# First values accumulated in the projection's banks, and the second head begun beside the first

## The chip, the cores and the metric

The kernel runs on one core of one Trainium2 chip. TensorE (PE in the profile) multiplies into PSUM; VectorE (DVE), ScalarE (ACT) and GpSimd (POOL) read PSUM or SBUF and do everything else; SyncE (SP) issues the transfers. Each engine takes its instructions strictly in the order of its own queue, and semaphores tie the queues together. The metric is the time of one execution in device microseconds; less is better. The kernel before takes 2423.03 us (median of three runs, 2422.2 to 2424.73).

## What is computed

Two layers of a transformer trunk over 512 latent tokens and 256 context tokens, 1024 features wide. Only the start of the first layer matters here:

```python
mx = (silu_c @ w_ada[i] + b_ada[i])             # modulation: shift, scale, gate (latent)
mc = silu_cc @ w_ada[i] + b_ada[i]              # the same for the context
hc = modulate(rmsnorm(h_ctx, norm1_g[i]), sc1, ac1)
hx = modulate(rmsnorm(x, norm1_g[i]), sx1, ax1)
px = hx @ w_in[i]                               # columns: conv | q | k | v | gates
q_x = apply_rope(rmsnorm(q_x, q_norm_g[i]), cos, sin)     # per head, two maps of 64
k_x = apply_rope(rmsnorm(k_x, k_norm_g[i]), cos, sin)
# attention: two softmax maps per head (8 heads), p1 - lam * p2, times the values
```

Context tokens get the norm but no rotation. After attention, a convolution branch, a merge, an output projection and an MLP follow, and then the second layer.

## The kernel before

Every matmul is made of three, so that float32 accuracy comes out of rounded operands: each operand is split into a rounded high part and a remainder (`split`, lines 75 to 77: ACT rounds, line 76; DVE or POOL subtracts, line 77), and `mm3` (lines 102 to 106) accumulates high*high, high*low and low*high. In the rows of the trace these are the lines L104, L105 and L106. Tokens lie in six tiles of 128: tiles 0 to 3 are latent, 4 and 5 context (`NTT` is 6). Features lie in eight tiles of 128 (`KT` is 8, index `k`).

**The prologue.** The input is normalized and transposed (L324, L329, L331), and the modulation weights come in slabs of 1 MB (`ada_slab`, L209 on: products L216 into `adaps`, copy L222, turn L225, reductions L228, bias L231; `ada_gain` is L240). The loop over `q` takes two slabs at a time, 4+q and q, which give shift and scale of the feature tiles 2q and 2q+1. For these two the modulated input is formed (L368 into `XN`) and split into `h1h` and `h1l`. `qk_part(k)` then accumulates the first head's queries and keys for feature tile `k` over all six token tiles. Each token tile has a PSUM bank of 512 float32 columns, `ps_qk[t]`, of which queries and keys use the left 256. Behind the loop the first value slab is loaded (`v_slab`, pair 0: heads 0 and 1), with its remainder subtracted on POOL, and the residual stream `X` is copied out to `xs_d` (3 MB) behind that load.

**The heads.** `qk_head(h)` is a generator. For each token tile, `project(t)` makes the matmuls (none for head 0, which takes `ps_qk`) and then copies the raw result out of its bank (L488, `rw`), squares it (L491, `sq`), reduces (DVE L493), adds epsilon and takes the power -1/2 on POOL (L494, L495), scales the keys (L496: DVE for latent tiles, POOL for context), and rotates: on POOL L505 (`ra`) and L509 (`rb`, two), added on DVE at L513 into `dup`; for context tiles POOL writes `dup` at L518. `turn(t)` transposes `dup` on PE (L529, `qkT`), copies it (ACT L533) and subtracts remainders (DVE L534, L536). `v_pair(pr)` makes the values of two heads, token tile by token tile, each with 24 matmuls into a bank of its own, and splits the result into `vh` and `vl`. `attend(h)` makes scores (L658, L660: `S`), their maxima (DVE L662), exponentials (ACT L667) and so on.

The order of the first layer's head phase is written by hand: two steps of head 0, two of the values, then four rounds of head 0, values, head 0. Then, for each head, `merge` interleaves `attend(h)` with fill work in a given ratio: the next head's `qk_head` and part of the next pair of values. For h = 0, four steps of head 1 are drawn ahead of it. On top of this program order a scheduler arranges instructions on each engine; the order quoted below is the one after that.

## Time and profile before

| what | value |
|---|---|
| median of three runs | 2423.03 us |
| the profiled execution | 2429.01 us |
| its span, first to last instruction | 2427.0 us |
| mean granted TensorE clock | 0.985 |
| PE, DVE, ACT, POOL busy | 96%, 56%, 39%, 29% |
| first value matmul begins; second score tile of head 1 begins | 60.92 us; 144.35 us |

The span's 2427.0 us and 2.0 us around it make the 2429.01 us of the profiled execution. All times inside the trace are counted from the start of the span. A row of a timeline gives start, duration, engine, line and operation, and in brackets the idle time of that engine just before, with what ended it. Instructions of a kind that follow each other closely stand in one row with their count.

### The profile page before, as it was taken

The numbers are of one execution on the slowest core, as the hardware profiler recorded it, in microseconds if no ns is written. First come the engines' busy times: TensorE is split into PE (matmuls) and PEld (weight loads), VectorE is DVE, ScalarE is ACT, GpSimd is POOL, SyncE is SP. The second block draws the span as 40 slices with busy tenths as digits, with TensorE's granted clock in tenths as the row PEclk, the third lists the DMA queues.
The fourth block names the chain that finished last, engine by engine and source line by source line (L and its number), as shares of the span: only waits on it lengthen the run. The fifth ranks groups of instructions, "written<-read, shape, count | busy, mean of one in ns | idle before, by whom it ended". The sixth has DMA issues, their size and how long they took to land.

```text
span 2427.0 us, 36997 instructions
## 1 busy us (share of the span) xinstructions
PE 2329.8 (96%) x15034; PEld 2065.2 (85%) x15034; DVE 1347.6 (56%) x2311; ACT 948.0 (39%) x1839; POOL 693.7 (29%) x1034
## 2 busy tenths in 40 slices
PE   7999998999999999999999998999999989999999
PEld 6889998878878988888888997999977769888887
DVE  6666776499657452222222356676759966433332
ACT  5455665522323242221312245555552323422331
POOL 2856765120000131120211256675630000200100
PEclk9999999999999999999999998999998999999999
DMA  8201101144445133333333221111114323232322
GB/s 291 68 27 44 45 27 60 42 134 128 155 135 172 53 105 112 114 122 116 110 122 101 69 75 53 42 42 43 43 59 137 126 70 122 87 103 89 104 87 70
DMA packets 222186, 224.79 MB, mean 93 GB/s; under 512 B 5872, under 2 KB 212160, under 8 KB 221888
## 3 DMA queue, kind: packets, MB, share of 16 engines
q1 hardware_dynamic: 222016, 222.43, 28.6%
q8 instruction: 118, 1.93, 0.3%
q14 instruction: 52, 0.43, 0.1%
HBM read 208.73 MB, written 13.67 MB: 92 GB/s over the span
## 4 chain that ended last, share of the span: by engine, by line
PE 79%; POOL 8%; DVE 7%; ACT 3%; issue 1%; DMA 1%; SPq 0%; POOLq 0%; ACTq 0%; DVEq 0%
PE r L104 6%; PE r L106 6%; PE f L104 6%; PE r L105 6%; PE f L105 6%; PE f L106 6%; PE gt L104 3%; PE gt L106 3%; PE gt L105 3%; PE adaps L216 2%; PE qk L104 2%; PE qk L105 2%; PE yc L113 2%; PE qk L106 2%; PE o L104 2%; PE o L106 2%
## 5 line engine op out<-in xcount | busy, mean ns | idle before, releaser
L104 PE MATMUL r<-fh,h_w 128*128 128x512 f32 (+1 forms) x832 | 285.5, 344 | 0.5 <-DVE X L1082 0.5
L104 PE MATMUL f<-h2h,h_w 128*128 128x512 f32 (+1 forms) x832 | 284.3, 345 | 1.3 <-ACT h2h L76 1.0
L105 PE MATMUL f<-h2l,h_w 128*128 128x512 f32 (+1 forms) x832 | 284.1, 343 | 1.1 <-POOL h2l L77 1.0
L105 PE MATMUL r<-fl,h_w 128*128 128x512 f32 (+1 forms) x832 | 283.2, 341 | 0.0
L106 PE MATMUL r<-fh,l_w 128*128 128x512 f32 (+1 forms) x832 | 283.2, 341 | 0.0
L106 PE MATMUL f<-h2h,l_w 128*128 128x512 f32 (+1 forms) x832 | 282.3, 341 | 0.0
L76 ACT ACTIVATE h_w<-r_w 128x1024 fp32r<-128x1024 f32 x128 | 128.8, 1053 | 312.4 <-PE r L105 131.0
L1151 POOL TENSOR_TENSOR fr<-fr 128x512 f32<-128x512 f32 (+1 forms) x104 | 93.3, 899 | 508.2 <-ACT fh L1150 508.2
L897 DVE SCALAR_TENSOR_TENSOR cacc<-z,cols,cacc 128x783 f32<-128x783 f32 (+1 forms) x240 | 203.7, 902 | 0.4
L104 PE MATMUL qk<-h_wqk,h1h 128*128 128x256 f32 x640 | 184.7, 291 | 7.8 <-ACT h1h L76 3.6
L105 PE MATMUL qk<-l_wqk,h1h 128*128 128x256 f32 x640 | 182.1, 286 | 0.0
L1082 DVE SCALAR_TENSOR_TENSOR X<-r,ad,X 128x512 f32<-128x512 f32 (+1 forms) x104 | 64.9, 627 | 210.3 <-PE r L106 210.2
L106 PE MATMUL qk<-h_wqk,h1l 128*128 128x256 f32 x640 | 178.7, 287 | 0.0
L104 PEld LDWEIGHTS f<-h2h,h_w 128*128 128x128 f32 x832 | 157.4, 190 | 25.0 <-ACT fh L1150 2.5
L104 PEld LDWEIGHTS r<-fh,h_w 128*128 128x128 f32 x832 | 157.6, 190 | 23.7 <-issue 3.7
L105 PEld LDWEIGHTS f<-h2l,h_w 128*128 128x128 f32 x832 | 158.3, 190 | 20.6 <-POOL h2l L77 2.5
L667 ACT ACTIVATE e<-S,st,rqk 128x768 f32<-128x768 f32 (+1 forms) x160 | 145.0, 909 | 75.5 <-POOL st L664 72.6
L106 PEld LDWEIGHTS f<-h2h,l_w 128*128 128x128 f32 x832 | 158.1, 190 | 17.6
L106 PEld LDWEIGHTS r<-fh,l_w 128*128 128x128 f32 x832 | 157.7, 190 | 17.8
L105 PEld LDWEIGHTS r<-fl,h_w 128*128 128x128 f32 x832 | 157.8, 190 | 17.0
L77 DVE TENSOR_TENSOR l_w<-r_w,h_w 128x1024 fp32r<-128x1024 f32 x106 | 126.2, 1223 | 79.5 <-ACT h_w L76 77.8
L1152 DVE TENSOR_TENSOR fl<-fr,fh 128x512 fp32r<-128x512 f32 (+1 forms) x104 | 62.5, 604 | 189.3 <-POOL fr L1151 189.2
(248 smaller groups left out, 6280.7 us busy)
## 6 DMA issues: line engine op xcount, KB each, us to landing
r_w<-in_w_mlp_dram SPq DMA_DIRECT2D x64, 1024.0 KB, 5.3
ada<-in_w_ada_dram SPq DMA_DIRECT2D x48, 1024.0 KB, 5.3
r_wqk<-in_w_in_dram SPq DMA_DIRECT2D x32, 512.0 KB, 5.2
r_wg<-in_w_in_dram SPq DMA_DIRECT2D x16, 1024.0 KB, 5.3
r_wv<-in_w_in_dram SPq DMA_DIRECT2D x8, 1024.0 KB, 5.4
r_wao<-in_w_attn_out_dram SPq DMA_DIRECT2D x8, 1024.0 KB, 5.2
r_wo<-in_w_out_dram SPq DMA_DIRECT2D x8, 1024.0 KB, 8.3
at_d<-uo SPq DMA_DIRECT2D x40, 128.0 KB, 1.7
```

The costliest lines, as they stand in the source:

```text
L76: nc.scalar.activation(out=hi, in_=src, func=AF.Copy)
L77: (lo_eng or nc.vector).tensor_tensor(out=lo, in0=src, in1=f32(hi), op=ALU.subtract)
L104: nc.tensor.matmul(ps, sh, mh, start=first, stop=False)
L105: nc.tensor.matmul(ps, sh, ml, start=False, stop=False)
L106: nc.tensor.matmul(ps, sl, mh, start=False, stop=last)
L113: nc.tensor.matmul(ps, w[j][:, k, m0 : m0 + P], a(k)[0][:, toks], start=k + j == 0, stop=False)
L216: nc.tensor.matmul(ps[32 * j : 32 * j + 32, :256], cvec[:, k, :], r[:, k, :], start=k < 4, stop=k >= 4, tile_position=(0, 32 * j))
L667: nc.scalar.activation(out=e[:, :nkey], in_=S[:, :nkey], func=AF.Exp, scale=R[:, t, m : m + 1], bias=st[:, m : m + 1], accum_out=st[:, 2 + ...
L897: nc.vector.scalar_tensor_tensor(out=ca[cc][:, :CV], in0=zt[cc][:, t : t + CV], scalar=wcol, in1=ca[cc][:, :CV], op0=ALU.mult, op1=ALU.add)
L1082: nc.vector.scalar_tensor_tensor(out=X[:, mb, g], in0=ps[:, :W], scalar=gate[:, s, mb : mb + 1], in1=X[:, mb, g], op0=ALU.mult, op1=ALU.add)
L1151: nc.gpsimd.tensor_tensor(out=r[:, :W], in0=r[:, :W], in1=r[:, :W], op=ALU.mult)
L1152: nc.vector.tensor_tensor(out=fl[mb][:, g], in0=r[:, :W], in1=f32(fh[mb][:, g]), op=ALU.subtract)
```

## The change

There are two parts.

First, the values of pair 0 are no longer made tile by tile in banks of their own. Their slab is loaded inside the modulation loop at q = 2, ahead of that turn's two modulation slabs. A new function `v_part` accumulates them, feature tile by feature tile, in the right half of the six banks `ps_qk[t]`, whose left half holds head 0's queries and keys: feature tiles 0 and 1 behind projection parts 4 and 5, the other six behind parts 6 and 7. Since the projection's first matmul has opened the bank, these begin with `start=False`. `v_pair(0)` then only splits the right halves into `vh` and `vl`.

Second, head 1's generator is made ahead of the hand-written order and four of its steps (three projections and more) are drawn there, one in each round where a tile of values stood; the loop over heads takes this generator on.

```diff
+    def v_part(ks):
+        w = first["v"]
+        for k in ks:
+            for t in range(NTT):
+                for a, b, e in ((hh, 0, False), (hh, 1, False), (hl, 0, k == KT - 1)):
+                    nc.tensor.matmul(ps_qk[t][:, 256:], a[:, k, t * P : t * P + P], w[b][:, k, :],
+                                     start=False, stop=e, skip_group_check=True)
+
     for q in range(4):
+        if q == 2:
+            first["v"] = v_slab(0, 0, nc.gpsimd)
         ada_slab(0, L, 4 + q)
         ada_slab(0, L, q)
...
             qk_part(2 * q - 1)
+        if q == 3:
+            v_part(range(2))
     qk_part(KT - 2)
     qk_part(KT - 1)
+    v_part(range(2, KT))
     first["ps"], first["w"] = ps_qk, w_qk
-    first["v"] = v_slab(0, 0, nc.gpsimd)
...
         def v_pair(pr):
+            pre = ps_qk if i == 0 and pr == 0 else []
...
             for t in range(NTT):
+                if pre:
+                    split(vh[:, t], vl[:, t], pre[t][:, 256:])
+                    yield 0.0
+                    continue
                 ps = mm_tile(f"v{i}_{pr}_{t}")
...
-            drain(part(head0, 2))
-            drain(part(v0, 2))
+            head1 = qk_head(1)
+            for _ in range(2):
+                drain(part(head0, 1))
+                drain(part(v0, 1))
             for _ in range(NTT - 2):
                 drain(part(head0, 1))
                 drain(part(v0, 1))
+                drain(part(head1, 1))
                 drain(part(head0, 1))
...
-                qk = qk_head(h + 1)
+                qk = head1 if h == 0 and not last else qk_head(h + 1)
```

The lines behind the new function move by 12 to 19 in the changed kernel: L368 becomes L380, L488 to L536 become L502 to L550, L658 becomes L677, L660 becomes L679. The value matmuls of pair 0 are L369.

On SP, the queue of loads at the end of the modulation, before:

```order
L81 DMA ada_1_410<-in_w_ada_dram 128x8x256
L81 DMA ada_6_478<-in_w_ada_dram 128x8x256
L81 DMA ada_2_496<-in_w_ada_dram 128x8x256
L81 DMA ada_7_564<-in_w_ada_dram 128x8x256
L81 DMA ada_3_582<-in_w_ada_dram 128x8x256
L90 DMA r_wv_0_686<-in_w_in_dram 128x8x256
L379 DMA xs_d_79<-X_92 128x6144
L88 DMA r_wqk_1_991<-in_w_in_dram 128x8x128 x2
```

and now:

```order
L81 DMA ada_1_410<-in_w_ada_dram 128x8x256
L90 DMA r_wv_0_478<-in_w_in_dram 128x8x256
L81 DMA ada_6_486<-in_w_ada_dram 128x8x256
L81 DMA ada_2_504<-in_w_ada_dram 128x8x256
L393 DMA xs_d_79<-X_92 128x6144
L81 DMA ada_7_572<-in_w_ada_dram 128x8x256
L81 DMA ada_3_590<-in_w_ada_dram 128x8x256
L88 DMA r_wqk_1_903<-in_w_in_dram 128x8x128 x2
```

The value slab passes four modulation slabs, and the copy of the residual passes the last two.

On POOL, from the split of the value slab on, before (`rqk` is the norm of a head's tiles, `l_` a weight's remainder; the first number in a name is the head, the next the tile):

```order
L77 TENSOR_TENSOR l_wv_0_689<-r_wv_0_686,h_wv_0_688 128x1024 x2
L494 TENSOR_SCALAR rqk_0_705<-rqk_0_705 128x4
L495 TENSOR_TENSOR rqk_0_705<-rqk_0_705,mhalf 128x4
L505 TENSOR_TENSOR ra_0_0_715<-rw_0_0_706,tC_120 128x256
L509 TENSOR_TENSOR rb_0_0_716<-rw_0_0_706,tS_121 128x4x32 x2
```

and now:

```order
L77 TENSOR_TENSOR l_wv_0_481<-r_wv_0_478,h_wv_0_480 128x1024 x2
L77 TENSOR_TENSOR l_wqk_1_907<-r_wqk_1_903,h_wqk_1_906 128x1024
L508 TENSOR_SCALAR rqk_0_849<-rqk_0_849 128x4
L509 TENSOR_TENSOR rqk_0_849<-rqk_0_849,mhalf 128x4
L77 TENSOR_TENSOR l_wv_1_1385<-r_wv_1_1382,h_wv_1_1384 128x1024
L519 TENSOR_TENSOR ra_0_0_859<-rw_0_0_850,tC_120 128x256
L523 TENSOR_TENSOR rb_0_0_860<-rw_0_0_850,tS_121 128x4x32 x2
```

The halves of head 1's projection weights and of the second value slab, which stood behind head 0's tiles 0 and 5, now stand ahead of and inside tile 0.

On PE, around the first scores, before (`qkT` are turns, `S` scores; head, tile):

```order
L106 MATMUL qk_1_1_1050<-h_wqk_1_994,h1l_335 128x256
L658 MATMUL S_0_0_0_1104<-qk_0_704 128x512
L660 MATMUL S_0_0_0_1104<-qk_0_704 128x512
L658 MATMUL S_0_0_1_1113<-qk_0_704 128x512
L660 MATMUL S_0_0_1_1113<-qk_0_704 128x512
L529 MATMUL qkT_0_4_1042<-cst,dup_0_4_900 128x128 x2
L529 MATMUL qkT_0_5_1090<-cst,dup_0_5_946 128x128 x4
L104 MATMUL qk_1_2_1127<-h_wqk_1_994,h1h_334 128x256
```

and now:

```order
L106 MATMUL qk_1_3_1124<-h_wqk_1_906,h1l_335 128x256
L543 MATMUL qkT_0_2_1080<-cst,dup_0_2_894 128x128 x4
L543 MATMUL qkT_1_0_1101<-cst,dup_1_0_947 128x128 x4
L543 MATMUL qkT_0_3_1109<-cst,dup_0_3_970 128x128 x4
L677 MATMUL S_0_0_0_1194<-qk_0_848 128x512
L679 MATMUL S_0_0_0_1194<-qk_0_848 128x512
L677 MATMUL S_0_0_1_1203<-qk_0_848 128x512
L679 MATMUL S_0_0_1_1203<-qk_0_848 128x512
L543 MATMUL qkT_0_4_1164<-cst,dup_0_4_1035 128x128 x2
L543 MATMUL qkT_1_1_1172<-cst,dup_1_1_1012 128x128 x4
```

Four projections of head 1 (tiles 0 to 3) and a turn of head 1 now stand ahead of the first scores, where two projections stood; head 0's turns 0_0 to 0_2, which lay among the value matmuls, come behind them. The rest of the first scores (the last 256 keys) stands behind the fifth projection, where it stood behind the third.

## The prediction

> **What bounds the kernel now.** I read the page's busy table and chain of waits first, then the table by stretches, and last the rows of the stretches that the change touches.
>
> ```profile
> span 2427.0 us, 36997 instructions
> PE 2329.8 (96%) x15034; PEld 2065.2 (85%) x15034; DVE 1347.6 (56%) x2311; ACT 948.0 (39%) x1839; POOL 693.7 (29%) x1034
> PE 79%; POOL 8%; DVE 7%; ACT 3%; issue 1%; DMA 1%; SPq 0%; POOLq 0%; ACTq 0%; DVEq 0%
> ```
>
> PE works 96% of the span, and the change leaves its matmuls as they are (13429 rows in both orders). So the change can only move the time in which PE waits. POOL is busy 29% on average, but it holds 8% of the chain: somewhere it sets the pace. The stretches say where (columns: PE, PEld, DVE, ACT, POOL busy, granted clock, DMA share, GB/s):
>
> ```profile
> 50.00:55.00 5.00, 2.91 (x25) 2.71 (x23) 4.90 (x7) 0.90 (x1) 4.70 (x2) 1.00 0.25 103
> 55.00:60.00 5.00, 3.54 (x29) 3.54 (x30) 3.69 (x9) 1.76 (x4) 0.00 (x0) 1.00 0.02 6
> 60.00:70.00 10.00, 10.00 (x85) 9.92 (x83) 4.76 (x7) 5.33 (x13) 6.67 (x8) 1.00 0.38 102
> 70.00:81.00 11.00, 9.77 (x83) 9.53 (x82) 7.98 (x18) 4.06 (x10) 9.44 (x15) 1.00 0.30 97
> 81.00:90.00 9.00, 7.93 (x61) 7.17 (x61) 4.23 (x8) 3.99 (x8) 8.76 (x11) 1.00 0.01 3
> 90.00:97.00 7.00, 5.98 (x35) 5.53 (x36) 3.50 (x9) 1.78 (x4) 5.81 (x9) 0.76 0.56 149
> 97.00:121.00 24.00, 22.32 (x174) 21.08 (x173) 21.29 (x41) 15.04 (x31) 20.81 (x37) 1.00 0.16 43
> 121.00:145.00 24.00, 23.12 (x185) 22.09 (x184) 13.10 (x29) 12.95 (x34) 6.64 (x21) 1.00 0.05 14
> ```
>
> From 62 to 121 us POOL is busy nearly throughout (9.44 of 11, 8.76 of 9, 20.81 of 24), and PE still loses only about 5 us there. PE is kept going because it has the first values' matmuls to do from 60.92 on, while POOL already normalizes and rotates head 0's tiles. The one large PE wait is in 50 to 60, and its cause stands in these rows of POOL, DVE, ACT and PE:
>
> ```profile
> 50.03 4.70 POOL L77 TENSOR_TENSOR l_wv<-r_wv,h_wv 128x1024 fp32r<-128x1024 f32 x2 [16.79 <-ACT h_wv L76]
> 50.14 2.31 DVE L231 TENSOR_TENSOR ad<-ad,cols 128x4 f32<-128x4 f32 x1
> 52.49 2.33 DVE L240 SCALAR_TENSOR_TENSOR A<-ad,cols 128x2 f32<-128x2 f32 x2
> 55.01 0.16 DVE L231 TENSOR_TENSOR ad<-ad,cols 128x4 f32<-128x4 f32 x1
> 56.47 0.39 PE L104 MATMUL qk<-h_wqk,h1h 128*128 128x256 f32 x1 [3.55 <-ACT h1h L76]
> 35.23 0.60 ACT L329 ACTIVATE XN<-nT 128x512 f32<-128x512 f32 x1 [0.79 <-PE nT L324]
> 37.19 0.17 DVE L231 TENSOR_TENSOR ad<-ad,cols 128x4 f32<-128x4 f32 x1
> ```
>
> A 128x4 add that takes 0.16 us takes 2.31 while POOL splits the wv slab, and the next DVE step waits for POOL's second half. PE then stands 3.55 us. The Trainium skill, "SBUF — State Buffer", section "Who interferes with whom", calls the port pair that VectorE and GpSimd share an exclusive lock; the trace agrees (4.70 us of POOL against 2.31 + 2.33 of DVE), and by that rule too an earlier split moves the block rather than ending it.
>
> **The change, part by part.** First, the early wv slab. Its load now stands where ada_6 stood. ACT's two h_wv halves come right behind its L329 copy (35.23 + 0.60), so POOL's split starts at about 37 and lasts to 41.7. DVE has just come to the L231 of the second modulation group (37.19). It is held to about 41.5, some 4.2 us late. PE has the ada_6 products ahead of what waits for this, so I take a PE wait of 3.9 us; bounds 0 and 4.7.
>
> The third group's wait was covered by the products of ada_7 and ada_3; these now come behind the value matmuls. The chain is in these rows:
>
> ```profile
> 45.16 0.38 PE L225 MATMUL adaps<-cst,adasb 128*128 128x128 f32 x2
> 45.92 0.16 DVE L231 TENSOR_TENSOR ad<-ad,cols 128x4 f32<-128x4 f32 x1
> 46.70 0.94 ACT L76 ACTIVATE h1h<-XN 128x512 fp32r<-128x512 f32 x2 [3.88 <-DVE XN L368]
> ```
>
> From the end of the turn (45.5) to the first half of h1h (about 47.3) it is 1.8 us, uncovered now. In the fourth group two turns stand side by side in front of the last projection parts, so the same chain with a second gain is some 2.4 us. I take 1.85 + 2.4; bounds 0 each and 4.4 together, or 9.1 with the first. The load of the residual copy also moves ahead of ada_7 and ada_3, but all of these bytes had landed soon after 50 us (the 50 to 55 row moves only 103 GB/s), and PE comes to those products at about 60: nothing.
>
> When do the values end? Rows of PE:
>
> ```profile
> 60.92 0.39 PE L104 MATMUL v<-h_wv,h1h 128*128 128x256 f32 x1
> 71.48 0.39 PE L104 MATMUL v<-h_wv,h1h 128*128 128x256 f32 x1 [1.23 <-DVE vl L77]
> 79.80 0.60 PE L529 MATMUL qkT<-cst,dup 128*128 128x128 f32 x4
> 80.95 0.28 PE L106 MATMUL v<-h_wv,h1l 128*128 128x256 f32 x1
> 88.14 0.40 PE L658 MATMUL S<-qk 128*128 128x512 f32 x1
> 96.46 0.28 PE L658 MATMUL S<-qk 128*128 128x256 f32 x1
> 144.35 0.50 PE L658 MATMUL S<-qk 128*128 128x512 f32 x1
> ```
>
> Before, the last value matmul gives way at 81.07. Three turns of head 0 lie among them (0.36 from one start to the next matmul, 1.1 in all), and the waits of 3.55 and 1.23. Without these it would be 75.2. With the new waits of 8.15 it is **83.3**. The prologue alone is thus no gain: 4.8 us of waiting goes, 8.15 comes.
>
> Second, and this carries the forecast: head 0's POOL work loses its cover. The copy of each tile out of its bank (raw q and k) now waits for the last matmul into that bank, and that is a value matmul. All six banks end within 1.8 us at 83.3, because the values run by feature tile. So POOL, which began head 0 at 62.62, begins at about 84. Its price per tile:
>
> ```profile
> 62.62 0.24 POOL L494 TENSOR_SCALAR rqk<-rqk 128x4 f32<-128x4 f32 x1 [7.88 <-DVE rqk L493]
> 62.94 1.03 POOL L495 TENSOR_TENSOR rqk<-rqk,mhalf 128x4 f32<-128x4 f32 x1
> 64.43 0.74 POOL L505 TENSOR_TENSOR ra<-rw,tC 128x256 f32<-128x256 f32 x1 [0.46 <-DVE rw L496]
> 65.14 0.88 POOL L509 TENSOR_TENSOR rb<-rw,tS 128x128 f32<-128x128 f32 x2
> 66.09 1.08 POOL L494 TENSOR_SCALAR rqk<-rqk 128x4 f32<-128x4 f32 x1
> 76.53 0.73 POOL L494 TENSOR_SCALAR rqk<-rqk 128x4 f32<-128x4 f32 x1
> 80.56 1.03 POOL L494 TENSOR_SCALAR rqk<-rqk 128x4 f32<-128x4 f32 x2
> 86.42 2.40 POOL L77 TENSOR_TENSOR l_wv<-r_wv,h_wv 128x1024 fp32r<-128x1024 f32 x1
> 89.14 0.72 POOL L518 TENSOR_TENSOR dup<-rw,gr 128x256 f32<-128x256 f32 x1
> 88.78 0.39 POOL L496 TENSOR_TENSOR rw<-rw,rqk 128x128 f32<-128x128 f32 x1
> ```
>
> A latent tile takes 3.47 (62.62 to 66.09) to 4.03 us (76.53 to 80.56); I take 3.7. POOL's new order is: norm of head 0's tile 0 (84.0 to 85.3); half of the second wv slab, for which ACT first rounds 2 us (86.5 to 88.9); the rest of tile 0 (to 90.6); then tiles 0_1, 0_2, 1_0, 0_3, 1_1, five at 3.7, to 109.1. Then context tile 0_4 mixed with 1_2: two L494 0.5, two L518 1.44, two L495 2.4, L496 0.4, L505 0.74, L509 0.88, in all 6.4; and 0_5 mixed with 1_3 up to its last dup, without the L509 pair, 5.5: **121.0**. Head 0's last turn, its copy and two differences take 0.3 + 0.6 + 0.85 by these rows:
>
> ```profile
> 84.23 0.60 ACT L533 ACTIVATE qk<-qkT 128x512 fp32r<-128x512 f32 x1 [0.67 <-PE qkT L529]
> 84.86 0.42 DVE L534 TENSOR_TENSOR qk<-qkT,qk 128x256 fp32r<-128x256 f32 x1 [0.65 <-ACT qk L533]
> ```
>
> So the last part of the first scores, at 96.46 before, comes at **122.8**, 26.3 later. PE has done more by then: the projections of head 1's tiles 3 and 4 (48 matmuls, 0.12 apart, 5.8) and three turns (1.1), 6.9 us that the later stretch no longer holds. Net 19.4. That PE has projections in this stretch does not help enough: from 83.3 it has four of them (11.5 us), the fourth behind a copy that stands on ACT behind head 0's first turn; the fifth stands behind the turns, and PE is in order. Of 39 us it works about 19.
>
> Third, what comes back: from 97 to 145 PE waits 2.6 us (24 - 22.32 and 24 - 23.12), partly for POOL, which has less left to do there. I take 2.4 back. From the second head's second score tile (144.35) on, the order is nearly the same, so what is late there stays late. **Sum: +19.4 - 2.4 = +17.** The profiled execution took 2429.0 (span 2427.0), 6 us above the median of the runs, so 2446 profiled and **2440** as a median.
>
> Least: the prologue's waits all hidden (-8.15) and tiles at 3.47 (-1.2), so +8. Most: waits of 9.1, tiles at 4.03 (+1.7), nothing regained, +24.
>
> **The rivals.** (1) Faster: head 1's projections cover head 0's chain, and the 36 value matmuls fill the wait of 3.55. Then PE loses neither 3.55 nor 1.23 nor the 2.1 it waits from 81 to 97: -6.9, 2416. It needs head 0's six tiles through POOL in the 11.5 us of four projections, under 2 us each, where no row shows less than 3.47. 8%.
>
> (2) The copies wait only for their own half of the bank. Then POOL starts when the last projection part ends, 60.92 - 3.55 + 8.15 + 4.3 (36 values) = 69.8, so at about 71.5 rather than 84, and the first scores come 12 us sooner: +5 to +7, 2429. For it: the two halves are different addresses. Against: copy and values use one bank tile, and the copy's wait in the order is on PE behind the values. 8%.
>
> (3) No change: POOL's idle time after 121 (6.64 busy of 24) takes up the delay. That holds for POOL, not for PE, whose score matmuls stand in order behind the turns. It needs PE waits of under 5 us in the head stretch. 8%.
>
> (4) The waiting slows the clock. In 90 to 97 the granted clock is 0.76, behind waits of a few tenths, yet 1.00 behind the wait of 3.55. If it fell in the starved stretch, the fifth projection and the turns ahead of the first scores (4 us of matmuls) would take up to twice as long: +4, 2444. [...] 13%.
>
> **How the numbers follow.** Forecast 63%: 2440, its own range 2430 to 2448. With the cases the range is 2428 to 2449: it leaves out rival 1, rival 3, and parts of the tails. A measurement of this kernel can tell about 0.2% (4.8 us) from no change. Faster 8%; same 10% (rival 3, and a piece of rival 2); slower 82%.
>
> **What would show it.** Right: POOL's first norm of head 0 at about 84 instead of 62.6; PE busy for only half of 84 to 122, its waits ended by DVE and POOL (dup, rw, qk); the last part of the first scores at 119 to 126; the score at 144.35 near 161; POOL's wv split near 37 with long DVE rows beside it, and PE's wait of 3.55 at 53 gone but one like it near 40. Wrong: raw copies of head 0 before the values end (rival 2), POOL tiles of under 3 us, or PE without waits from 84 to 122 (rival 1).

## The result, and the profile after

The change takes 2457.07 us (median of four runs, 2453.31 to 2458.68) against 2422.89 us for the kernel before, run beside it (four runs, 2422.2 to 2424.73). The ratio is 1.0129, 95% interval 1.0117 to 1.0141: slower by 1.3%. The forecast was 2440 with a range up to 2449. The sign was right; the forecast rise of 17 us was half of the 34 that came.

The profiled execution of the change took 2453.31 us (2429.01 before). Its busy table and its chain of waits:

```profile
span 2451.5 us, 37011 instructions
PE 2334.7 (95%) x15034; PEld 2066.7 (84%) x15034; DVE 1353.2 (55%) x2311; ACT 946.7 (39%) x1839; POOL 690.5 (28%) x1034
PE 77%; POOL 8%; DVE 8%; ACT 4%; DMA 2%; issue 1%; SPq 0%; ACTq 0%; POOLq 0%; DVEq 0%
```

The span is 24.5 us longer, and PE is busy only 4.9 us more. The table by stretches (us, then PE, PEld, DVE, ACT, POOL busy, granted clock, DMA share, GB/s) shows where:

```profile
50.00:55.00 5.00, 3.16 (x26) 2.95 (x25) 3.92 (x11) 1.76 (x4) 0.00 (x0) 1.00 0.28 91
60.00:70.00 10.00, 7.96 (x77) 6.18 (x78) 4.49 (x16) 2.53 (x6) 0.00 (x0) 1.00 0.04 11
70.00:81.00 11.00, 11.00 (x94) 11.00 (x93) 1.22 (x1) 2.01 (x2) 2.44 (x1) 1.00 0.40 109
90.00:97.00 7.00, 4.65 (x35) 4.41 (x35) 3.86 (x9) 2.47 (x6) 5.85 (x10) 0.92 0.55 148
97.00:121.00 24.00, 11.73 (x50) 9.09 (x50) 12.60 (x30) 7.83 (x18) 20.95 (x33) 0.57 0.00 0
121.00:145.00 24.00, 21.95 (x161) 20.34 (x160) 18.61 (x34) 13.41 (x27) 15.90 (x29) 0.95 0.17 45
```

From 55 to 70 POOL now stands idle (6.67 us of work in 60 to 70 before). From 97 to 121 PE works 11.73 of 24 us where it worked 22.32, on 50 matmuls instead of 174, at a granted clock of 0.57 instead of 1.00. The rows of PE, first its prologue waits, then the last value matmul, then the end of the first scores:

```profile
43.06 0.51 PE L106 MATMUL qk<-h_wqk,h1l 128*128 128x256 f32 x2 [3.49 <-DVE h1l L77]
52.05 0.39 PE L104 MATMUL qk<-h_wqk,h1h 128*128 128x256 f32 x1 [1.84 <-ACT h1h L76]
65.98 0.39 PE L104 MATMUL qk<-h_wqk,h1h 128*128 128x256 f32 x1 [1.84 <-ACT h1h L76]
...
83.23 0.28 PE L369 MATMUL qk<-h_wv,h1l 128*128 128x256 f32 x1
...
110.42 0.76 PE L677 MATMUL S<-qk 128*128 128x512 f32 x1 [1.87 <-DVE qk L550]
116.42 0.69 PE L543 MATMUL qkT<-cst,dup 128*128 128x128 f32 x2 [2.43 <-POOL dup L532]
119.16 0.69 PE L543 MATMUL qkT<-cst,dup 128*128 128x128 f32 x2 [2.05 <-POOL dup L532]
119.50 0.56 PE L104 MATMUL qk<-h_wqk,h1h 128*128 128x256 f32 x1
120.29 0.41 PE L104 MATMUL qk<-h_wqk,h1h 128*128 128x256 f32 x1
120.93 0.41 PE L104 MATMUL qk<-h_wqk,h1h 128*128 128x256 f32 x1
...
126.26 0.35 PE L677 MATMUL S<-qk 128*128 128x256 f32 x1 [0.82 <-DVE qk L550]
...
168.55 0.50 PE L677 MATMUL S<-qk 128*128 128x512 f32 x1
```

The second score tile of head 1 stands at 168.55 instead of 144.35, 24.2 us late, and the span is 24.5 longer, so the loss arises ahead of that tile. (That the two agree to 0.3 is chance: two more traces of the change, below, have the same stretch some 3 us later and spans 23.9 and 24.1 longer.) The rows of L104 at 120.29 and 120.93 are three matmuls apart, 0.21 us from one start to the next; the forecast counted 0.12. Rows of POOL and one of ACT show where PE's wait comes from. ACT's first copy of head 0 waits 5.53 us until a value matmul (L369) has ended. Head 0's first norm starts at 83.84 instead of 62.62, and a tile then takes 3.9 us (90.66 to 94.56):

```profile
36.60 4.68 POOL L77 TENSOR_TENSOR l_wv<-r_wv,h_wv 128x1024 fp32r<-128x1024 f32 x2 [3.62 <-ACT h_wv L76]
81.75 0.38 ACT L502 ACTIVATE rw<-qk 128x256 f32<-128x256 f32 x1 [5.53 <-PE qk L369]
83.84 0.24 POOL L508 TENSOR_SCALAR rqk<-rqk 128x4 f32<-128x4 f32 x1 [5.05 <-DVE rqk L507]
90.66 0.73 POOL L508 TENSOR_SCALAR rqk<-rqk 128x4 f32<-128x4 f32 x1
91.47 1.05 POOL L509 TENSOR_TENSOR rqk<-rqk,mhalf 128x4 f32<-128x4 f32 x1
92.93 0.72 POOL L519 TENSOR_TENSOR ra<-rw,tC 128x256 f32<-128x256 f32 x1 [0.41 <-DVE rw L510]
93.61 0.86 POOL L523 TENSOR_TENSOR rb<-rw,tS 128x128 f32<-128x128 f32 x2
94.56 0.72 POOL L508 TENSOR_SCALAR rqk<-rqk 128x4 f32<-128x4 f32 x1
```

**Waiting and slower work, apart.** The second row of L715 (L734 in the change), in which squares of head 0's output are summed, begins at 143.10 before and at 167.30 after. PE's busy time from 30 us to there, of the kernel before and of the change:

```profile
30.00:143.10 113.10, 103.26 (x854) 95.86 (x847) 76.83 (x166) 54.08 (x122) 61.86 (x96) 0.98 0.34 111
```

```profile
30.00:167.30 137.30, 109.85 (x850) 99.27 (x846) 76.52 (x165) 53.87 (x122) 60.17 (x96) 0.91 0.28 91
```

PE is idle for 113.10 - 103.26 = 9.84 us before and 27.45 after: **17.6 more**. It is busy for 103.26 and 109.85: **6.6 more**, for the same matmuls to within the few records that are missing (854 and 850), at a clock of 0.91 instead of 0.98. The first figure is near the forecast's +17; the second is nowhere in its sum. The two are a way of counting, not two prices: a matmul that runs slower inside a wait costs nothing, it only makes the wait shorter. This pair, idle and busy up to the second L715 row, is given for every run below; I call that row's start the mark.

### The profile page after: what moved, and what is told of

Same layout as the page of the kernel before. It is cut to its first block, busy times and chain, and to the rows that moved or that the text cites. A ratio compares the mean times of both kernels' runs of the same rounds, so it can differ in the third digit from the quotient of the medians.

```text
span 2451.5 us, 37011 instructions
## 1 busy us (share of the span) xinstructions
PE 2334.7 (95%) x15034; PEld 2066.7 (84%) x15034; DVE 1353.2 (55%) x2311; ACT 946.7 (39%) x1839; POOL 690.5 (28%) x1034
## 4 chain that ended last, share of the span: by engine, by line
PE 77%; POOL 8%; DVE 8%; ACT 4%; DMA 2%; issue 1%; SPq 0%; ACTq 0%; POOLq 0%; DVEq 0%
PE r L104 6%; PE r L106 6%; PE r L105 6%; PE f L104 6%; PE f L105 6%; PE f L106 6%; PE gt L104 3%; PE gt L105 3%; PE gt L106 3%; PE adaps L216 2%; PE qk L104 2%; PE qk L105 2%; PE qk L106 2%; POOL rqk L509 2%; PE yc L113 2%; PE o L104 2%
## 5 line engine op out<-in xcount | busy, mean ns | idle before, releaser
L104 PE MATMUL r<-fh,h_w 128*128 128x512 f32 (+1 forms) x832 | 285.4, 344 | 0.5 <-DVE X L1104 0.5
L104 PE MATMUL f<-h2h,h_w 128*128 128x512 f32 (+1 forms) x832 | 284.2, 344 | 1.3 <-ACT h2h L76 1.0
L104 PE MATMUL qk<-h_wqk,h1h 128*128 128x256 f32 x640 | 184.6, 290 | 10.6 <-ACT rw L502 6.3
L104 PEld LDWEIGHTS f<-h2h,h_w 128*128 128x128 f32 x832 | 157.3, 190 | 25.1 <-ACT fh L1172 2.5
L104 PEld LDWEIGHTS r<-fh,h_w 128*128 128x128 f32 x832 | 157.7, 190 | 23.8 <-issue 3.7
```

Of the source, the lines that this page charges most:

```text
L104: nc.tensor.matmul(ps, sh, mh, start=first, stop=False)
```

## The experiments

The kernel before, the change and all 18 further runs, with PE's idle and busy time from 30 us to the mark in the traced execution. "Scores" is the time from the last value matmul to the last part of head 0's first scores (43.0 in the change).

| run | median, us | ratio, 95% | mark | idle | busy | scores |
|---|---|---|---|---|---|---|
| before | 2422.89 | | 143.10 | 9.84 | 103.26 | |
| before again | 2427.83 (one) | | 143.34 | 10.24 | 103.10 | |
| change | 2457.07 | 1.0129, 1.0117 to 1.0141 | 167.30 | 27.45 | 109.85 | 43.0 |
| change again | 2457.43 | 1.0125, 1.0111 to 1.0138 | 170.15 | 27.38 | 112.77 | |
| change, third | 2452.86 (one) | | 170.25 | 27.43 | 112.82 | |
| values only | 2450.86 | 1.0105, 1.0082 to 1.0127 | 165.23 | 26.27 | 108.96 | |
| head 1 only | 2442.33 | 1.0071, 1.0044 to 1.0097 | 158.00 | 16.78 | 111.22 | |
| values by tile | 2451.82 | 1.0109, 1.0082 to 1.0136 | 167.23 | 24.65 | 112.58 | |
| wv split on DVE | 2448.70 | 1.0094, 1.0073 to 1.0116 | 164.09 | 24.45 | 109.64 | 42.5 |
| three edits together | 2441.17 | 1.0056, 1.0042 to 1.0071 | 158.75 | 21.16 | 107.59 | |
| PE kept warm | 2452.53 | 1.0111, 1.0098 to 1.0124 | 170.23 | 20.95 | 119.28 | 42.2 |
| rotation on DVE | 2445.70 | 1.0077, 1.0052 to 1.0102 | 169.53 | 28.35 | 111.18 | 42.4 |
| ring of 7 | 2455.55 | 1.0123, 1.0107 to 1.0139 | 168.00 | 27.50 | 110.50 | 43.0 |
| ring of 7, rotation on DVE | 2445.85 | 1.0085, 1.0069 to 1.0101 | 167.86 | 28.07 | 109.79 | 42.3 |
| norm one tile ahead | 2452.97 | 1.0120, 1.0105 to 1.0135 | 165.15 | 25.13 | 110.02 | 38.2 |
| norm ahead, rotation on DVE | 2449.14 | 1.0096, 1.0082 to 1.0110 | 168.60 | 23.43 | 115.17 | 37.1 |
| before, wv split on DVE | 2431.28 | 1.0020, 1.0011 to 1.0029 | 143.11 | 9.98 | 103.13 | |
| before, wv and rotation on DVE | 2430.25 | 1.0010, 0.9998 to 1.0022 | 139.72 | 7.49 | 102.23 | |
| before, 16 useless transposes | 2429.55 | 1.0017, 1.0007 to 1.0026 | 144.04 | 9.29 | 104.75 | |
| before, 32 useless transposes | 2436.35 | 1.0038, 1.0023 to 1.0053 | 152.12 | 11.73 | 110.39 | |

Each ratio is to runs of the kernel before made beside it, whose median lay between 2422.89 and 2427.08; so ratios are compared, not medians of different rows. The three traces of the change have marks 3 us apart and idle times within 0.1, so a difference of marks under some 3 us is not read as an effect.

### The two parts, each alone

Values only: the change with the hand-written order of before, so that head 1 begins inside the merge again.

```diff
-            head1 = qk_head(1)
-            for _ in range(2):
-                drain(part(head0, 1))
-                drain(part(v0, 1))
+            drain(part(head0, 2))
+            drain(part(v0, 2))
...
-                drain(part(head1, 1))
...
-                qk = head1 if h == 0 and not last else qk_head(h + 1)
+                qk = qk_head(h + 1)
```

> The values stay in the projection's banks, the second head is begun where it was before. Theory A (the lost cover: POOL can start head 0 only when the values end, at 83.8 us in the profile of the change, and PE has nothing left to do meanwhile): still slower than the kernel before by 14 to 24 us, 2437 to 2447. POOL has head 0's tiles alone (six at 3.5 to 3.9 us and half a wv slab), so head 0's last turn comes at about 110 instead of 124. Theory B (beginning head 1 beside head 0 is what costs, since its tiles go between head 0's on POOL): nearly all comes back, 2423 to 2429.

Head 1 only: the same three places of the order turned the other way in the kernel before, values as before.

> The values are made as before, tile by tile in banks of their own; only the second head is begun beside the first. Theory A: POOL starts at 62.6 as before, under the value matmuls, and PE has values and projections to do: 2423 to 2432. Theory B: most of the loss is here, 2440 to 2457.

The values alone come to 2450.86 (idle +16.4 of the change's +17.6), above the 2437 to 2447 of theory A; head 1 alone comes to 2442.33 (idle +6.9), which theory B had named. Neither reading had foreseen that each part costs alone, and that the two together cost little more than the values do. In the run with head 1 only, head 0's POOL work starts in time (63.25), so a late start of head 0 isn't its cause. These are rows of PE in it:

```profile
97.19 0.50 PE L658 MATMUL S<-qk 128*128 128x512 f32 x1 [1.62 <-DVE qk L536]
101.14 0.66 PE L529 MATMUL qkT<-cst,dup 128*128 128x128 f32 x2 [2.67 <-DVE qk L536]
111.58 0.36 PE L104 MATMUL qk<-h_wqk,h1h 128*128 128x256 f32 x1 [2.23 <-DVE qk L536]
```

Head 1's tiles share POOL and DVE with head 0's, so head 0's turns come later, and PE, which is in order, has no values left to do while it waits. Busy time rises by 8.0 us besides, at a granted clock of 0.91 up to the mark instead of 0.98.

### Values token tile by token tile, and the split on DVE

Values by tile: `v_part(range(2, KT))` goes over token tiles outside and feature tiles inside, so that the banks end one after the other.

```diff
-        for k in ks:
-            for t in range(NTT):
+        steps = [(k, t) for k in ks for t in range(NTT)]
+        if ks[0] == 2:
+            steps = [(k, t) for t in range(NTT) for k in ks]
+        for k, t in steps:
```

> As the change, but the values of feature tiles 2 to 7 are accumulated token tile by token tile, so that the first bank is complete after 18 of these 108 matmuls. Theory A: POOL's first norm of head 0 at about 74 instead of 83.8, the first scores about 10 us sooner, and 9 to 14 us less than the change: 2443 to 2448. Theory B or C (the early split of the wv slab holding VectorE): no difference, 2454 to 2459.

It missed: head 0's first norm came at 82.11 where 74 was expected, and the median, 2451.82, lies between the two readings. Part of this is the trace: its values end at 86.65, as in the second and third trace of the change (86.22 and 86.08), where the first norm comes at 86.83 and 86.69. Beside these it is 4.6 us sooner. The rest stands on ACT, where the copies out of the banks stand behind the rounding of head 1's weights, whose load lands late:

```profile
77.44 2.01 ACT L76 ACTIVATE h_wqk<-r_wqk 128x1024 fp32r<-128x1024 f32 x2 [6.95 <-DMA r_wqk<-in_w_in_dram]
79.36 0.37 ACT L505 ACTIVATE rw<-qk 128x256 f32<-128x256 f32 x1
```

This order on ACT is not owed to the early start of head 1: the rounding stands ahead of the first copy as well in the runs that begin head 1 as before (77.33 in values only, 69.55 in three edits together).

Wv split on DVE: the change with the remainder of the early value slab subtracted on DVE, so that POOL doesn't hold DVE out near 37.

```diff
-            first["v"] = v_slab(0, 0, nc.gpsimd)
+            first["v"] = v_slab(0, 0)
```

> As the change, but the remainder of the first wv slab is subtracted on VectorE (two ops of about 1.3 us) instead of POOL (4.7 us). Theory A: the PE wait of 3.5 us near 40 shrinks to about 1, and head 0's chain starts that much sooner: 1 to 3 us less than the change, 2454 to 2456. Theory C (the early split is the main cost): 8 us or more less, under 2449.

PE's wait of 3.49 falls to 0.52:

```profile
41.71 0.50 PE L106 MATMUL qk<-h_wqk,h1l 128*128 128x256 f32 x2 [0.52 <-DVE h1l L77]
```

The values end at 80.57 instead of 83.23, and idle time up to the mark falls by 3.0 us (27.45 to 24.45), about what that wait lost. This term of the prediction was therefore a cause, and its size right. The median fell further, to 2448.70, which is theory C's "under 2449" (ratio 1.0094 beside the change's 1.0129, or some 8 us). The trace has only 3.0 us of waits for it; where the other 5 come from is not shown.

Three edits together: values by tile, the split on DVE, head 1 begun as before.

> The change with three edits: values by token tile, wv remainder on VectorE, head 1 begun where it was before. POOL can begin head 0 near 78 (ACT does head 1's projection weights first, when they land), 5 us sooner than in the change but 15 later than before. Theory A: better than the change by 12 to 20 us but still slower than the kernel before by 8 to 16, 2432 to 2441. If the values' place were neutral and only the two side effects cost (the split on POOL, head 1 beside head 0), it would be at 2420 to 2427.

The first norm starts at 74.23, the last part of the first scores begins at 106.76, and the median is 2441.17: half of the loss is back, as the expectation had it. It is the best form of early values that ran, and still 0.56% slower than before.

### The clock

PE kept warm: the change with some 80 useless transposes behind the turns of heads 0 and 1, into a bank that no one reads.

```diff
+                if i == 0 and turn_tile and h < 2:
+                    for g in range(16):
+                        nc.tensor.transpose(state["dm"][:, :P], d[:, g % 4].rearrange("p a d -> p (a d)"), ident)
```

> The change with 16 extra transposes of no use behind each of five turns in the starved stretch (80 in all, 7 us at full clock), where PE waits for POOL anyway. Theory D: the granted clock from 97 to 121, 0.63 and 0.50 in the profile of the change, rises to 0.8 or more, the fifth projection takes 2.9 instead of 4.6 us, and the rest of the first scores comes 1 to 3 us sooner, for 1 to 4 us less than the change. If the slow clock costs nothing there, the rest of the first scores stays at 126 or comes up to 2 later.

The granted clock rises, as this run's table by stretches shows (97 to 110 had 0.63 in the change, 110 to 121 had 0.50):

```profile
97.00:110.00 13.00, 10.94 (x94) 10.25 (x92) 8.21 (x19) 4.62 (x12) 11.20 (x19) 1.00 0.02 5
110.00:121.00 11.00, 5.29 (x32) 3.75 (x32) 6.91 (x16) 3.69 (x10) 9.95 (x18) 0.81 0.01 2
```

The scores come 42.2 us after the values instead of 43.0, where 1 to 3 less was expected; the median, 2452.53, is 4.9 below that of the change run beside it, with intervals that overlap. So in 97 to 110 the low clock follows from PE's idleness and can be lifted by filling it, and that gains little: there POOL and DVE set the pace. At the place where a gain was expected the filler did not reach. The fifth projection, which in the change starts at 119.50, starts here at 121.71 behind waits of 2.9 and 2.2 us and again has its matmuls 0.21 us apart; it takes 5.3 us, where 2.9 was expected. So this run does not show what a fast fifth projection is worth.

Change again, change a third time and before again are unchanged kernels:

> The change itself, run beside the following three. Theory A (lost cover) with D (TensorE's clock falls to half in some stretches after a wait, at places that differ from one execution to the next): the second score tile of head 1 again near 168.5 us (half a clock window more or less, 166 to 172), the median 2450 to 2458, its executions spread over 4 us and more. If the clock had no part, the profile would show 168.5 within 0.3 and the executions would agree within 1 us.

> The change once more, for a third trace. Theory D: the waits until the second score tile of head 1 (those over 0.25 us) again 26.9 us within 0.2, while that tile's start lies anywhere from 168 to 172 by where the clock was low.

> The kernel before, for a second trace. Theory D: waits of 9.6 us until the second score tile of head 1 as in the first, its start 142 to 147 by where the clock was low: 144.35 with one low window of 3.3 us, 142.9 without it.

They came in the main as theory D has it. Up to the mark, idle time is nearly the same in all traces of a kernel (27.45, 27.38, 27.43; 9.84, 10.24). Busy time isn't: 109.85, 112.77, 112.82 for the change. The extra 3 us come from two low-clock stretches in the prologue that the first trace doesn't have. From 30 to 60 us, first the first trace of the change, then the second, which has the same waits:

```profile
30.00:60.00 30.00, 23.54 (x216) 20.43 (x216) 17.93 (x43) 10.09 (x22) 5.23 (x3) 1.00 0.76 270
```

```profile
30.00:60.00 30.00, 23.52 (x189) 20.55 (x186) 17.93 (x43) 10.10 (x22) 5.25 (x3) 0.89 0.76 270
43.09 0.50 PE L106 MATMUL qk<-h_wqk,h1l 128*128 128x256 f32 x2 [3.51 <-DVE h1l L77]
44.15 0.41 PE L104 MATMUL qk<-h_wqk,h1h 128*128 128x256 f32 x1
...
53.57 0.38 PE L104 MATMUL qk<-h_wqk,h1h 128*128 128x256 f32 x1 [1.84 <-ACT h1h L76]
54.38 0.41 PE L104 MATMUL qk<-h_wqk,h1h 128*128 128x256 f32 x1
```

From 44.15 to 47.56 and from 54.38 to 57.79 the second trace has its matmuls 0.21 us apart; those right behind, at 48 and 58 us, stand 0.12 apart. Each low stretch begins about 1 us after a wait has ended, one of 3.51 and one of 1.84 us; in the first trace the same two waits slow nothing. So the length of a wait alone does not decide. The Trainium skill, "TensorE: Matmul & The Clock Gate", section "What's actually happening", says that the clock follows an activity window of some 3.4 us that runs freely, and that the moment at which the clock rises depends on where in this window the first matmul lands. The two low stretches, 3.4 us each, agree with that length. That where a wait falls in the window decides whether it slows the clock is an inference; no run here shows the window itself.

### What sets the pace of the starved stretch

A tile took 3.9 us between 84 and 122, of which POOL works 3.4 (the four durations from 90.66 on, 0.73 + 1.05 + 0.72 + 0.86), and the forecast had counted POOL's durations. Five runs of the change ask what sets this pace. Rotation on DVE: the products `ra` and `rb` of heads 0 and 1 move from POOL (1.58 us a tile) to DVE (shown for `ra`; `rb` alike).

```diff
-                    nc.gpsimd.tensor_tensor(
+                    (nc.vector if i == 0 and h < 2 else nc.gpsimd).tensor_tensor(
```

> The change with the rotation's products of heads 0 and 1 in the first layer (three ops per latent tile, 1.6 us on POOL) on VectorE. Theory A: POOL is the pace of the starved stretch, so a latent tile takes 2.2 to 3 us instead of 3.9, head 0's last turn comes at 112 to 119 instead of 124, and the time falls by 5 to 12 us against the change, to 2445 to 2452. If POOL were not the pace (the copies or the turns were), the rest of the first scores would stay within 2 us of 126 to 129.

Ring of 7: seven buffers in place of four for `sq`, `ra`, `rb` and the other tiles of tag "sc" in the first layer (shown for `sq`); then both edits together.

```diff
-                sq = ap.tile([P, 4, QK], F32, tag="sc", name=f"sq{i}_{h}_{t}", bufs=4)
+                sq = ap.tile([P, 4, QK], F32, tag="sc", name=f"sq{i}_{h}_{t}", bufs=7 if i == 0 else 4)
```

> The change, with seven buffers instead of four in the ring that holds a tile's squares and its two rotation products (first layer only), so that the next tile's squares need not wait for the tile before. Theory A (the ring of four makes head 0's and head 1's tiles go one at a time): a tile takes about 3.0 to 3.3 us instead of 3.9 between 84 and 122, POOL's own time per tile being 2.9 (0.24 + 1.03 + 0.74 + 0.88); the last part of the first scores comes 4 to 6 us sooner after the end of the values than the 43.0 of the change, and the second score tile with it. Rival B (POOL's own load sets the pace with its share of two heads): tiles stay at 3.8 to 4.0 and the first scores within 1.5 us of the change's.

> The change with both edits: seven buffers in the ring, and the rotation products of heads 0 and 1 on DVE instead of POOL. Theory A (ring and POOL are two limits, one behind the other): with both gone the tiles come at 2.3 to 3 us and the first scores 8 to 12 us sooner after the values' end than in the change (43.0). Rival B (the chain through ACT, DVE and POOL is long because its steps stand behind other work in the queues, with or without the ring): 40 to 43.

The scores' 43.0 us became 42.4, 43.0 and 42.3. The ring of `sq`, `ra` and `rb` is not the limit, and POOL's load is not the limit by itself, though the ring's run alone would have fitted that rival. (The medians of the two runs with the rotation on DVE, 2445.70 and 2445.85, do lie some 10 us below the change by their ratios, and the first of them in theory A's range. By the traces most of this gain lies behind the mark: from the mark to the end of the span it is 2274 and 2276 us in these runs and 2281 to 2284 in the three traces of the change. Why is not shown.) What holds the tiles stands in the rows of ACT and DVE in the run with both edits:

```profile
91.82 0.42 ACT L505 ACTIVATE sq<-rw 128x256 f32<-128x256 f32 x1
...
93.36 0.29 DVE L510 TENSOR_TENSOR rw<-rw,rqk 128x128 f32<-128x128 f32 x1 [0.91 <-POOL rqk L509]
93.68 0.43 DVE L519 TENSOR_TENSOR ra<-rw,tC 128x256 f32<-128x256 f32 x1
94.03 0.48 DVE L523 TENSOR_TENSOR rb<-rw,tS 128x128 f32<-128x128 f32 x2
94.43 0.41 DVE L507 TENSOR_REDUCE rqk<-sq 128x4 f32<-128x256 f32 x1
```

The last row reduces the next tile's squares. They had been ready since 92.24 on ACT (the first row), but the reduction stands behind the scaling of the tile before (L510), which waits for POOL's power. One tile is in the chain at a time: reduction, POOL's two steps, scaling, rotation, then the next. In the change itself POOL's queue has the same form: norm, rotation, norm, rotation (the rows from 90.66 on above), with 0.41 us of waiting for DVE in most tiles. So the last two runs turn this order round: the norm of a tile is written ahead of the scaling and rotation of the tile before, with six raw copies (tag "rw") instead of four; once alone, once with the rotation on DVE. `rotate` now holds the scaling and rotation of a tile:

```diff
+                if i == 0 and h < 2:
+                    old, held[:] = list(held), [rotate]
+                    for f_ in old:
+                        f_()
```

> The change with another order of the same work: the norm of a tile (copy, squares, reduction, epsilon, power) of heads 0 and 1 is written ahead of the scaling and rotation of the tile before, and the raw copies get six buffers instead of four. Theory (POOL and DVE take their queues in order, and each tile's reduction and norm stand behind the rotation of the tile before, so that a tile's whole chain, 0.73 + 1.05 + 0.41 of waiting on DVE + 0.72 + 0.86, passes before the next begins): a tile takes 3.1 to 3.5 us instead of 3.9 and the last part of the first scores comes 36 to 40 us after the end of the values instead of 43.0; the median is 2446 to 2453. Rival (the stretch is paced by something else again, as with the ring and POOL's load): 42 us or more.

> As the run before, with the rotation products of heads 0 and 1 on DVE besides. Theory: the two edits together break the chain and take 1.6 us of each tile from POOL, so a tile takes 2.4 to 3.0 us and the first scores end 29 to 36 us after the values; the median is 2434 to 2444. Rival (something else paces): 40 us or more, as the rotation on DVE alone with 42.35. A kernel at or under the one before is expected by neither, since head 0 still begins 21 us later.

With the order turned and the rotation left on POOL, the scores come 38.2 us after the values, within the expectation; the median, 2452.97, is at its upper end, and its interval overlaps that of the change. From 97 to 110, first in the change and then in that run, POOL's last gaps close:

```profile
97.00:110.00 13.00, 5.63 (x29) 4.65 (x28) 8.09 (x21) 5.53 (x13) 10.67 (x17) 0.63 0.00 0
```

```profile
97.00:110.00 13.00, 4.39 (x22) 3.03 (x21) 10.70 (x23) 5.62 (x13) 12.34 (x22) 0.64 0.02 6
```

So the queue order was the first limit (POOL busy 10.67 of 13 us), and POOL's load is the next (12.34 of 13). One rival is left: both runs also have six raw copies, and no run has these with the old order. In the change the fifth raw copy and those after it do wait on ACT for a tile's rotation (3.49 us at 90.61). Against it stands that the waits of POOL between 90 and 110 are put down to the scaling on DVE (L510), one of 0.25 to a reduction, and none to a copy. With the rotation on DVE besides, DVE is full (12.61 of 13) and the scores gain only 1.1 us more: 37.1 where 29 to 36 was expected, and a median of 2449.14 where 2434 to 2444 was. The expectation had not counted DVE's load.

### Small gains and small delays in the kernel before

Before, wv split on DVE: the same edit as above in the kernel before. Before, wv and rotation on DVE: head 0's rotation products moved as well.

> The kernel before with one edit: the remainder of the first wv slab is subtracted on VectorE instead of POOL. By the lock as the profile of before shows it (3.55 us of PE waiting at 52.9), that wait shrinks to 0.5 to 2, and POOL starts head 0 as much sooner: 1.5 to 3.5 us less than before, 2420 to 2423. If the wait at 52.9 had another cause, no difference.

> The kernel before with the wv remainder and head 0's rotation products on VectorE. If POOL is what PE waits for in 80 to 121 us and the split is what it waits for at 52.9, most of these 9 us of waits go: second score tile of head 1 at 138 to 142 instead of 144.35, 2416 to 2422. Rival: the matmuls that are left in order, or VectorE (21.3 of 24 us busy in 97 to 121), become the bound, and it stays within 2 us of the kernel before, 2422 to 2428.

Both medians missed. In the first, PE's wait of 3.55 falls to 1.31, as expected, and head 0 starts 3.5 us sooner, but the mark stays at 143.11 and idle time up to it at 9.98: the lead is given back in other waits. The median is even 5.9 us higher (2431.28 against 2425.41), though the traced execution, 2424.59, is the shortest of its twelve; why is not shown. In the second, idle time falls to 7.49 and the second score tile of head 1 comes at 140.97, within the expected 138 to 142, and the timed median still is not lower (2430.25 against 2427.08). By its median no version that ran beats the kernel before.

Before with 16 or 32 useless transposes ahead of head 0's fourth turn, into a bank that no one reads:

```diff
+                if i == 0 and h == 0 and t == 3:
+                    dm = state["mi"]("pad")
+                    for g in range(16):
+                        nc.tensor.transpose(dm[:, :P], d[:, g % 4].rearrange("p a d -> p (a d)"), ident)
```

> The kernel before, with 16 useless transposes (their bank is read by no one) ahead of head 0's fourth turn. This delays PE there by a known amount, about 16 times 0.09 to 0.12 us, 1.4 to 1.9 us in the trace, and changes nothing else. Theory A (a delay near the start costs the timed median what it costs the trace): median 1.0 to 2.0 us above before's. Rival B (timed executions amplify or swallow it, because the low-clock windows fall elsewhere): the median moves by over 4 us or by under 0.

> As the run with 16, with 32: 2.8 to 3.8 us of delay in the trace. Theory A: median 2.5 to 4 us above before's and about twice that of 16. Rival B: by over 6 us or under 1.

The expectations were wrong in saying that nothing else changes: the scheduler also moved scores and turns behind the insertion, and with 32 by far more (mark +9.0). So they can't tell a pure delay. With 16, the trace is 0.9 us later at the mark and 5.8 over its span (2432.8 against 2427.0), and the median 4.7 (interval 1.7 to 6.3). With 32 it is 9.0 at the mark and 8.3 over the span (2435.3), and the median 11.5 (5.6 to 12.8). The spans lie within the intervals of the medians; of the marks, that of the run with 16 does not. So what a delay costs at the mark can differ from what it costs at the end by about 5 us, and finer than that these runs settle nothing.

## Why the prediction was right in sign and too small

**The bound, and the prologue: right.** The waits of 3.9, 1.85 and 2.4 measured 3.49, 1.84 and 1.84, with one of 0.51 besides; the values end at 83.23 (forecast 83.3). POOL's split of the value slab stands at 36.60 (forecast 37) with the long DVE rows beside it. With this split on DVE the first wait falls to 0.52, so its cause is shown. The fourth group's chain was no longer than the third's: 1.84, not 2.4.

**Head 0 loses its cover: right, and the main cause.** POOL's first norm came at 83.84 (forecast 84), 21 us later than before, since the copies wait for the last value matmul into each bank. The values alone bring 16.4 of the 17.6 us by which PE's idle time grows. Head 1's early start brings 6.9 by itself; the forecast had it only inside POOL's sum and as work done ahead, never as a cost of its own. With the three edits together the first norm came at 74.23, about half as late, and about half of the loss was back; how much of it is each edit's is not told apart. The reason given for the tile's price was incomplete: it was POOL's durations (3.47 to 4.03, taken as 3.7; 3.9 measured). POOL works 3.4 of these 3.9 us, but the order of the queues, one tile at a time, holds much the same pace when the rotation is taken off POOL. The number was nearly right, and the reason would have misled a reader who then took work off POOL.

**The sum: the first step that failed, 7.3 of the 17 us that were missing.** The forecast let the first scores end 26.3 us late, subtracted 6.9 for work done ahead and 2.4 for waits regained later: +17. The rows by stretch, from the values' end to the last part of the first scores and from there to the tile at 144.35 or 168.55, first before and then in the change:

```profile
81.07:96.46 15.39, 13.30 (x90) 12.09 (x89) 7.56 (x16) 5.46 (x10) 13.96 (x19) 0.89 0.26 70
96.46:144.35 47.89, 45.33 (x359) 43.14 (x357) 33.99 (x68) 27.62 (x65) 27.72 (x56) 1.00 0.10 29
```

```profile
83.35:126.26 42.91, 27.15 (x163) 23.82 (x161) 23.39 (x49) 15.19 (x34) 34.98 (x52) 0.72 0.09 25
126.26:168.55 42.29, 38.89 (x297) 36.20 (x297) 29.13 (x57) 23.70 (x56) 18.77 (x42) 1.00 0.12 32
```

The last part of the first scores came at 126.26, 29.8 late, so 3.5 more than forecast. POOL's last `dup` is done at 122.36 + 0.73 = 123.1 instead of 121.0, which is 2.1 of it: the five latent tiles took 4.0 us each (90.66 to 110.56) where 3.7 was counted, and the two context tiles 12.5 where 11.9 was. The projection at 119.50 takes 4.6 us (to 124.08) for 24 matmuls, most of them 0.21 apart, where 24 at 0.12 take 2.9. It ends 1.0 after the `dup` and holds back the turn; the other 0.4 lies in the turn, its copy and the differences.

The 2.4 did not come back, and 1.3 more were lost (29.8 - 6.9 + 1.3 = 24.2). From 126.26 to 168.55 PE waits 3.4 us, at a clock of 1.00, where it waited 2.56 before. The waits for POOL's `dup` are gone from there, but new ones for DVE (0.83 at 141.85) and ACT (0.88 at 160.47, 0.58 at 161.88) stand in their place.

That all waits together grew by 17.6, as the +17 has it, is partly luck. Up to the first scores PE waits 15.8 us where the forecast's terms make it some 18 (39.5 us from 83.3 to 122.8, less 13.3 of work that was there before, 1.1 for turns that moved there and 6.9 of head 1), because slower matmuls (27.15 us busy, at a clock of 0.72, where the terms make it some 21) fill part of the waiting; behind them it waits 3.2 more than forecast. The two misses nearly cancel. So the 6.6 us by which the same matmuls took longer are not a cost of 6.6: where PE waits for POOL anyway, slow matmuls cost nothing. The place where they were on the path is the fifth projection, and there they cost about 1 us by the rows, an estimate that no run tests. The price for it was in the trace of before, where the matmuls in 93 to 95 stand 0.21 apart at a clock of 0.50; it belonged into the sum instead of a rival of 13%.

The bound of +24 does not follow from its own terms either: 17, with 0.95 for the prologue's waits, 1.7 for the tiles and 2.4 not regained, make 22, and the trace came out above that.

**From the profiled execution to the median: the larger step that failed, 9.8 us.** The forecast took 6 us off, because the profiled execution of before lay 6 above the median. For the change the traced executions (2453.31, 2452.67, 2452.86) lie some 4 us below the median. So 6 were taken off where 4 had to be added. One profiled execution was no measure of a kernel's offset, and not even of the kernel before: a second trace of it took 2427.83 us beside a median of 2427.08, and its median moved between 2422.89 and 2427.08 from one set of runs to the next. Why the untraced executions of the change take 4 us longer than the traced ones stays open; the runs with a known delay did not settle it.

**The rivals.** Faster, because head 1's projections cover head 0: no, PE idles 12.3 of the 24 us from 97 to 121. Copies that wait for their own half of the bank: no, the first copy, at 81.75, waits for a value matmul. No change, because POOL's idle time takes it up: no. POOL did work 15.90 us instead of 6.64 from 121 to 145, and PE was late all the same. The clock: it did fall (0.57 in 97 to 121), beside the forecast instead of in place of it, and of the 4 us that the rival gave it the rows show about 1 on the path.

## What to carry to other kernels

Before work is moved ahead, ask what it was covering where it stood: here the values were what PE did while another engine prepared the first head, and pulling them forward left a hole of 16 us, and adding a competitor beside them one of 7. When a forecast leaves PE half idle for long, count the matmuls right behind that stretch at the lower clock too, as a term of the sum; those inside it cost nothing as long as another engine is later. Don't carry the offset of one profiled execution from one kernel to another. And when a chain over several in-order queues runs one tile at a time, look at which row of the next tile stands behind which wait of this one, before an engine's load or a ring of buffers is blamed.

## What the runs showed of the hardware that was not expected

Whether the clock falls is not tied to the length of one wait. Waits of 3.49 and 1.84 us left it at 1.00 in one trace; in the next trace of the same kernel a low stretch of 3.4 us followed each, and 30 to 60 us stood at 0.89. A stretch of waits of 2 to 3 us with short work between them (97 to 121) stood at 0.57 in the first. Up to the mark, idle time repeated to 0.1 us between three traces of the change and busy time only to 3 us. The spans of the three traces agree within 0.6 us all the same (2451.5, 2450.9, 2451.1), so this does not explain why timed executions spread. The kernel before, in 15 runs side by side, spread from 2421.79 to 2430.63, so an edit worth under about 5 us had to be read from idle and busy time in the trace; the medians did not tell it.
